# Attention by summation by parts: products replaced by differences of values, the last value added on the way out of PSUM

## The chip, the core and the metric

The program runs on one core of one Trainium2 chip. The metric is device time of one execution in microseconds; the kernel before takes 2888.41 us (median of three runs, 2887.97 to 2892.59). The core has five engines that work at once: PE (TensorE, matrix products, with its weight loads PEld), DVE (VectorE), ACT (ScalarE), POOL (GpSimd) and SP, which here only issues transfers. Each takes its own instructions in order and waits on semaphores for the others.

## What is computed

A decoder trunk of two layers over 1040 positions (16 learned ones and 1024 given) of width 1024: a Mamba-2 mixer with a conv FFN, and then a layer of stick-breaking attention with a conv FFN. The change is in the attention alone, 16 heads of 64 columns. Cut to what matters:

```
logits   = q k^T / 8                                  # for s < t only
log_keep = log_sigmoid(-logits)                       # 0 where s >= t
later    = reversed exclusive cumulative sum of log_keep over s
w        = exp(log_sigmoid(logits) + later)           # 0 where s >= t
out      = w v
```

So the weight of position s is b(s) times the product of all k(s') with s' > s, where b = sigmoid(logit) and k = sigmoid(-logit) = 1 - b, and k is 1 where s >= t. With P(s), the product of k from s to the end, the weight is b(s) P(s+1). As b = 1 - k, it is also P(s+1) - P(s).

## The kernel before

The attention works on 8 pairs of heads. The 1040 positions are cut into 9 chunks of 116 (the last has 112), and these into 3 tiles of three chunks (348, 348 and 344 positions). For each pair there are 18 steps: chunk i of queries against key tile jj, from the chunk's own tile down to tile 0. A step (`weigh`) has these pieces, with the names that rows of the profile show:

- PE: four matmuls `lg` (two heads, queries and keys in two parts each) into a PSUM tile of two banks, which there is once (twice for the last nine steps of the last pair).
- ACT: two sigmoids out of `lg`, with the query's factor as scale (`rt[2]` and `rt[1]`): k into `kp` and b into `bt` (L1398).
- POOL: sets the column behind the last of `kp` to 1 (L1393); where the tile is the chunk's own, it puts 1 into `kp` and 0 into `bt` at s >= t (L1403).
- DVE: two scans that run backward over `kp` and leave the products in it (L1407, one a head, starting from the product that the step before ended with), and then the product `bt` times `kp` shifted by one column (L1408).

Three steps later `turn` transposes the weights on PE (`wT`, L1421, into a ring of three PSUM banks) and ACT copies them out (`wt`, L1425). For every second chunk `values` then multiplies them with the values (`po`, L1436), ACT copies the result out (`o`, L1443) and sends it to memory for the layer behind.

The values get there so: a projection `pj` (L164 to L166) gives a tile of them with channels on partitions, ACT copies it out (`v`, L1324), and two steps later `place` turns it on PE (`pv`, into the same ring of three banks) and DVE multiplies it with the token's norm factor `rt[0]` on the way out (L1365). Keys (L1322) are multiplied by that factor `r` straight out of PSUM instead.

The projections of the next pair (queries, keys, values, 24 matmuls per kind and tile, in halves of 12) are put between the steps by hand: `halves` says which half stands at which step, and the last pair has such work only up to its step 7. In the attention the order of PE, DVE, ACT and POOL is that in which the program is written. Outside of it a scheduler sets the order. Behind the attention follows the output projection (`acc`), and then the second FFN.

Of the kernel before, what the change touches and what calls it, by code (L numbers as in the profile page):

```python
# [68 lines left out]
class Trunk:  # L69
# [1199 lines left out]
    def heads(self, u, p, pool):  # L1269
# [4 lines left out]
        class Pair:  # L1274
# [4 lines left out]
            def load(me, kind):  # L1279

                src, gain = {"k": (a["w_kv"][p], "kv_norm"), "q": (a["w_q"][p], "sb_norm"), "v": (a["w_kv"][PAIRS + p], "kv_norm")}[kind]
                w32 = self.wp.tile([P, 1024], F32, tag="w32", name=self.nm("w32"))
                nc.sync.dma_start(w32, src)
                if kind == "k":
                    me.ks = [self.Q("k", F32R), self.Q("k", F32R)]
                elif kind == "v":
                    me.v = pool.tile([P, 9, P], F32, tag="v", name=self.nm("v"), bufs=2)

                def scale_halves():
                    for x in range(2):  # L1290
                        v = w32[:, D // 2 * x : D // 2 * (x + 1)].rearrange("p (k c) -> p k c", c=P)
                        g = self.par(gain, KD // 2 * x, KD // 2).unsqueeze(2).to_broadcast([P, KD // 2, P])
                        nc.vector.tensor_tensor(v, v, g, op=ALU.mult)

                def part_halves():
                    me.w[kind] = [self.wp.tile([P, 1024], F32R, tag=t, name=self.nm(t)) for t in ("wh", "wl")]
                    halves = [[t[:, D // 2 * x : D // 2 * (x + 1)] for t in (w32, *me.w[kind])] for x in range(2)]
                    for w, wh, _ in halves:
                        nc.scalar.activation(wh, w, AF.Copy)
                    for w, wh, wl in halves:  # L1300
                        nc.vector.tensor_tensor(wl, w, wh.bitcast(F32), op=ALU.subtract)

                return [scale_halves, part_halves]

            def half(me, kind, j, h):
# [18 lines left out]
                nc.scalar.activation(t[:, :n], ps[:, :n], AF.Copy)  # L1324
                me.late.append((j, t))
# [29 lines left out]
            def place(me):  # L1355

                todo, me.old, me.late = me.old, me.late, []
                for j, t in todo:
# [5 lines left out]
                    for x, y, m in ((0, 3, CB),) if j < 2 else ((0, 2, CB), (2, 3, CH[8][1])):  # L1364
                        nc.vector.tensor_tensor(v[:m, 3 * j + x : 3 * j + y], pv[:m, x * P : y * P].rearrange("p (c d) -> p c d", d=P),  # L1365
                                                self.rt[0][:m, 3 * j + x : 3 * j + y].unsqueeze(2).to_broadcast([m, y - x, P]), op=ALU.mult)
# [3 lines left out]
    def token_factors(self, r, pool):  # L1370

        nc = self.nc
        self.rt = [pool.tile([P, 9], F32, tag=f"rt{x}", name=self.nm("rt"), bufs=1) for x in range(3)]
        for j, (s0, _) in enumerate(TT):
# [4 lines left out]
            for x, y, m in ((0, 3, CB),) if j < 2 else ((0, 2, CB), (2, 3, CH[8][1])):  # L1379
                src = ps[:m, : 3 * P].rearrange("p (c d) -> p c d", d=P)[:, x:y, 0]  # L1380
                for t, scale in zip(self.rt, (1.0, SCALE, -SCALE)):
                    nc.vector.tensor_scalar(t[:m, 3 * j + x : 3 * j + y], src, scale, None, op0=ALU.mult)

    def weigh(self, i, jj, qd, ks, prev, pool, ps):
# [6 lines left out]
        kp = pool.tile([P, 2, TW], F32, tag="kp", name=self.nm("kp"), bufs=3)  # L1391
        bt = pool.tile([P, 2, TW], F32, tag="bt", name=self.nm("bt"), bufs=4)
        nc.gpsimd.memset(kp[:nt, :, m : m + 1], 1.0)  # L1393
# [3 lines left out]
        for t, r in ((kp, self.rt[2]), (bt, self.rt[1])):  # L1397
            nc.scalar.activation(t[:nt, :, :m], ps[:nt, :, :m], AF.Sigmoid, scale=r[:nt, i : i + 1])  # L1398
        if jj == j:

            for t, fill in ((kp, 1.0), (bt, 0.0)):
                own = t[:nt, :, c0 : c0 + nt]
                nc.gpsimd.affine_select(out=own, in_=own, compare_op=ALU.is_gt, fill=fill, base=0, pattern=[[0, 2], [-1, nt]], channel_multiplier=1)  # L1403
        for a in range(2):
            rev = kp[:nt, a, : m + 1][:, ::-1]
            init = 1.0 if jj == j else prev[0][:nt, a, 0:1]
            nc.vector.tensor_tensor_scan(rev, rev, self.one[:nt].to_broadcast([nt, m + 1]), init, ALU.mult, ALU.mult)  # L1407
        nc.vector.tensor_tensor(bt[:nt, :, :m], bt[:nt, :, :m], kp[:nt, :, 1 : m + 1], op=ALU.mult)  # L1408
        prev[0] = kp
        return [bt[:, a] for a in range(2)]  # L1410

    def turn(self, i, jj, bt, wt):
# [4 lines left out]
        for a in range(2):  # L1417
            pt = self.sm("wT")
            for x, c in enumerate(blocks):
                ns = CH[c][1]  # L1420
                nc.tensor.transpose(pt[:ns, x * CB : x * CB + nt], bt[a][:nt, x * CB : x * CB + ns], self.ident[:nt, :nt])  # L1421
# [5 lines left out]
    def values(self, p, chunks, v, os, od):  # L1427
# [10 lines left out]
        for b, (i, _) in enumerate(chunks):  # L1438
# [4 lines left out]
            nc.scalar.activation(os[p][:, c0 : c0 + nt], po[:, b * CB : b * CB + nt], AF.Copy)  # L1443
# [3 lines left out]
    def attention(self, u, pool):  # L1447
# [15 lines left out]
        def flush(n):  # L1463
            if ready and (ready[-1][1] % 2 or ready[-1][1] == 8):
                p = ready[0][0]
                self.values(p, [(i, wts.pop((p, i))) for _, i in ready], pairs[p].v, os, od)
                ready.clear()
            if len(turns) > n:
                p, i, jj, bt = turns.pop(0)
                if jj == i // 3:  # L1470
                    wts[p, i] = [self.Q("wt")[:, : 9 * CB].rearrange("p (c t) -> p c t", t=CB) for _ in range(2)]
                self.turn(i, jj, bt, wts[p, i])
# [14 lines left out]
        for p in range(PAIRS):  # L1487
            prev = None
            for n, (i, jj) in enumerate(steps):
# [7 lines left out]
                bt = self.weigh(i, jj, now[0].qd[i // 3], now[0].ks, prev, pool, ps)  # L1497
# [14 lines left out]
                turns.append((p, i, jj, bt))  # L1512
# [182 lines left out]
```

## Time and profile before

| | us |
|---|---|
| median of the runs | 2888.41 |
| the profiled execution | 2887.39 |
| its span | 2885.7 |
| attention's first step (first `lg`) | at 1562 |
| last step's `po` begins | at 2079 |
| PE busy over the span | 2825.6 (98%) |
| DVE busy over the span | 2108.5 (73%) |
| ACT busy over the span | 1638.6 (57%) |
| POOL busy over the span | 664.1 (23%) |

Times in rows are microseconds from the start of the span. A row of a group names the line, the engine, the operation, output and inputs by the program's names, the count, and then the busy time, the mean of one in ns, and the idle time before it with what ended it. Matmuls are pipelined, so that PE's busy time holds some waiting, and short pieces of PE work look longer than the room they take. A row of a window gives its two ends, its length, for each engine the busy time with the count of instructions, and then PE's granted clock as a share of full speed, the share of the DMA engines and GB/s. A pair takes 65.6 us between the pairs in the middle.

### The profile page before, as it was taken

Reading aid. Unit: us, or ns where it says so; the run is one execution under the profiler, and the core shown is the slowest. Engines: PE = TensorE matmul, PEld = TensorE weight load, DVE = VectorE, ACT = ScalarE, POOL = GpSimd, SP = SyncE. Lnnn points to the kernel's source line nnn. Section 1 sums busy time; section 2 is a strip of 40 time slices with the busy share of each in tenths; the row PEclk is TensorE's granted clock in tenths of the full one; section 3 lists DMA queues with packets and bytes.
Section 4 is the critical chain, followed back from the end, with each engine's and each line's share of the span. In section 5 each row is a group of like instructions: output and inputs, shape, how many; then the busy total and the mean of one; then the engine's idle time right before and its main releaser. Section 6 shows DMA issues by size and latency. Waiting matters only on the chain.

```text
span 2885.7 us, 55788 instructions
## 1 busy us (share of the span) xinstructions
PE 2825.6 (98%) x21808; PEld 2706.5 (94%) x21808; DVE 2108.5 (73%) x3872; ACT 1638.6 (57%) x3203; POOL 664.1 (23%) x662
## 2 busy tenths in 40 slices
PE   8999999999999999999999999999999999999998
PEld 5989898989999999999999999999898999999888
DVE  5685868776587656568987888888769565657895
ACT  5576767773255555555435776777736555555442
POOL 0000000000005666650000111221101766662000
PEclk9999999999999999999999999999999999999999
DMA  6233333314221222226142222222341222225331
GB/s 169 79 111 87 117 94 110 106 57 157 86 95 67 80 76 81 76 97 212 53 136 79 64 62 67 67 62 57 132 152 52 88 75 80 78 78 190 110 110 59
DMA packets 134135, 274.76 MB, mean 95 GB/s; under 512 B 16464, under 2 KB 68304, under 8 KB 133872
## 3 DMA queue, kind: packets, MB, share of 16 engines
q1 hardware_dynamic: 128560, 260.26, 28.4%
q10 hardware_dynamic: 4048, 6.36, 0.6%
q0 software_dynamic: 1264, 4.57, 0.4%
q8 instruction: 172, 2.82, 0.4%
q14 instruction: 91, 0.75, 0.1%
HBM read 203.02 MB, written 53.21 MB: 89 GB/s over the span
## 4 chain that ended last, share of the span: by engine, by line
PE 73%; DVE 8%; issue 5%; ACT 5%; POOL 1%; DMA 0%; DVEq 0%; POOLq 0%; ACTq 0%; SPq 0%
PE p L166 10%; PE p L164 10%; PE p L165 10%; PE acc L166 8%; PE acc L165 8%; PE acc L164 8%; PE pj L164 4%; PE pj L165 4%; PE pj L166 4%; PE po L1436 2%; PE lg L1396 2%; PE wT L1421 2%; DVE kp L1407 1%; ACT D L614 1%; DVE bl L917 1%
## 5 line engine op out<-in xcount | busy, mean ns | idle before, releaser
L164 PE MATMUL pj<-uh,wh 128*128 128x348 f32 (+2 forms) x1536 | 502.8, 328 | 7.3 <-DVE xbc L292 6.1
L165 PE MATMUL pj<-ul,wh 128*128 128x348 f32 (+2 forms) x1536 | 495.5, 323 | 0.0
L166 PE MATMUL pj<-uh,wl 128*128 128x348 f32 (+2 forms) x1536 | 492.6, 321 | 0.0
L164 PE MATMUL p<-bh,fh 128*128 128x262 f32 (+1 forms) x1408 | 400.1, 285 | 8.5 <-DVE p L1041 4.7
L165 PE MATMUL p<-bl,fh 128*128 128x262 f32 (+1 forms) x1408 | 401.3, 285 | 0.4
L166 PE MATMUL p<-bh,fl 128*128 128x262 f32 (+1 forms) x1408 | 399.8, 285 | 0.3 <-DVE fl L972 0.3
L165 PE MATMUL p<-bl,wh 128*128 128x262 f32 (+1 forms) x1056 | 301.4, 285 | 1.5 <-DVE bl L917 1.5
L164 PE MATMUL p<-bh,wh 128*128 128x262 f32 (+1 forms) x1056 | 301.7, 286 | 1.0 <-ACT bh L916 1.0
L166 PE MATMUL p<-bh,wl 128*128 128x262 f32 (+1 forms) x1056 | 302.1, 286 | 0.0
L164 PEld LDWEIGHTS pj<-uh,wh 128*128 128x128 f32 x1536 | 289.2, 188 | 12.6 <-issue 7.8
L165 PEld LDWEIGHTS pj<-ul,wh 128*128 128x128 f32 x1536 | 289.6, 189 | 1.8 <-issue 0.6
L166 PEld LDWEIGHTS pj<-uh,wl 128*128 128x128 f32 x1536 | 289.0, 188 | 0.5
L164 PEld LDWEIGHTS p<-bh,fh 128*128 128x128 f32 x1408 | 268.1, 191 | 9.8 <-DVE p L1041 5.1
L292 DVE SCALAR_TENSOR_TENSOR c<-p,params,c 128x260 f32<-128x260 f32 (+1 forms) x440 | 208.2, 482 | 92.1 <-ACT c L288 90.2
L165 PEld LDWEIGHTS p<-bl,fh 128*128 128x128 f32 x1408 | 267.4, 190 | 1.6 <-DVE bl L917 1.4
L166 PEld LDWEIGHTS p<-bh,fl 128*128 128x128 f32 x1408 | 267.4, 190 | 0.7 <-DVE fl L972 0.5
L972 POOL TENSOR_TENSOR fl<-x,fh 128x1024 fp32r<-128x1024 f32 x80 | 192.5, 2406 | 253.3 <-ACT fh L971 253.3
L1041 DVE TENSOR_TENSOR p<-p,ft 128x262 f32<-128x262 f32 (+1 forms) x176 | 76.5, 436 | 215.3 <-ACT ft L1038 124.2
L165 PE MATMUL acc<-gl,wh 128*128 128x260 f32 (+1 forms) x672 | 211.1, 319 | 0.0
L166 PE MATMUL acc<-gh,wl 128*128 128x260 f32 (+1 forms) x672 | 208.3, 319 | 0.0
L165 PEld LDWEIGHTS p<-bl,wh 128*128 128x128 f32 x1056 | 202.2, 191 | 2.1 <-DVE bl L917 2.1
L164 PE MATMUL acc<-gh,wh 128*128 128x260 f32 (+1 forms) x672 | 204.0, 319 | 0.0
(313 smaller groups left out, 7507.0 us busy)
## 6 DMA issues: line engine op xcount, KB each, us to landing
w<-in_w_up SPq DMA_DIRECT2D x92, 512.0 KB
w<-in_w_down SPq DMA_DIRECT2D x44, 512.0 KB
w<-in_w_in SPq DMA_DIRECT2D x40, 512.0 KB
E<-ea_d SPq DMA_DIRECT2D x32, 464.0 KB
D<-acs_d SPq DMA_DIRECT2D x32, 420.5 KB
g<-c SPq DMA_DIRECT2D x88, 130.0 KB
g<-c SPq DMA_DIRECT2D x88, 128.0 KB
b<-g SPq DMA_DIRECT2D x16, 520.0 KB
```

Of the source, the lines that this page charges most:

```text
L164: mm(out, wh, uh, start=first, stop=False, skip_group_check=joins)
L165: mm(out, wh, ul, start=False, stop=False, skip_group_check=joins)
L166: mm(out, wl, uh, start=False, stop=last, skip_group_check=joins)
L292: nc.vector.scalar_tensor_tensor(to, ps[:, o + i : o + i + n], wcol(i), out, op0=ALU.mult, op1=ALU.add)
L614: nc.scalar.activation(dk[:, i], dk[:, i], AF.Relu, scale=-1.0, bias=self.cols[:n, 1, cc, h0 + i : h0 + i + 1])
L917: tt(hl[1], x, hl[0].bitcast(F32), op=ALU.subtract)
L972: (self.nc.vector if b < 2 else self.nc.gpsimd).tensor_tensor(lo[:, :n], t, hi[:, :n].bitcast(F32), op=ALU.subtract)
L1041: add = lambda o, x, y: tt(o[:, :N], x[:, :N], y[:, :N], op=ALU.add)
L1396: nc.tensor.matmul(ps[:nt, a, :m], part[:, c0 : c0 + nt], ks[a][:, s0 : s0 + m], start=x == 0, stop=x == 1)
L1407: nc.vector.tensor_tensor_scan(rev, rev, self.one[:nt].to_broadcast([nt, m + 1]), init, ALU.mult, ALU.mult)
L1421: nc.tensor.transpose(pt[:ns, x * CB : x * CB + nt], bt[a][:nt, x * CB : x * CB + ns], self.ident[:nt, :nt])
L1436: nc.tensor.matmul(po[64 * a : 64 * a + 64, w], v[: CH[c][1], c, 64 * a : 64 * a + 64], wt[a][: CH[c][1], c, :nt], start=x == 0, stop=x == ...
```

## The change

The sum of (P(s+1) - P(s)) v(s) over s is summed by parts: it is v at the last position minus the sum of P(s) (v(s) - v(s-1)), with v(-1) = 0. Since a row's P is 1 from s = t on, the last position of the query's own chunk serves as the last for its whole chunk. So the products P themselves, as the scan leaves them, are transposed and multiplied with v(s-1) - v(s), and v of the chunk's last position, which is a column of 128 channels, is added as the bias of ACT's copy out of PSUM.

In `weigh` this leaves out `bt`: its sigmoid, its POOL select, and the DVE product; the column of ones and its memset go too. `kp` has 6 buffers in place of 3 (and of 4 for `bt`). For the values, DVE multiplies the projection by `r` out of PSUM, where ACT copied before, POOL puts the last value of the tile ahead into column 0, DVE subtracts neighbours into another tile (`dv`), and POOL copies three columns (`ends`) aside for the bias. Those differences are turned on PE as the values were, and ACT copies them out where DVE multiplied by `rt[0]`. One table of token factors is left of three.

```
                 elif kind == "v":
                     me.v = pool.tile([P, 9, P], F32, tag="v", name=self.nm("v"), bufs=2)
+                    me.ends = pool.tile([P, 9], F32, tag="ends", name=self.nm("ends"), bufs=2)
...
-                nc.scalar.activation(t[:, :n], ps[:, :n], AF.Copy)
-                me.late.append((j, t))
+                front = me.ends[:, 3 * j - 1 : 3 * j] if j else self.zero[:, :1]
+                nc.gpsimd.tensor_copy(t[:, :1], front)
+                nc.vector.tensor_tensor(t[:, 1 : n + 1], ps[:, :n], u[KD][:, o:e], op=ALU.mult)
+                d = self.tmp("dv")
+                nc.vector.tensor_tensor(d[:, :n], t[:, :n], t[:, 1 : n + 1], op=ALU.subtract)
+                for i in range(3):
+                    last = CB * i + CH[3 * j + i][1]
+                    nc.gpsimd.tensor_copy(me.ends[:, 3 * j + i : 3 * j + i + 1], t[:, last : last + 1])
+                me.late.append((j, d))
...
-                        nc.vector.tensor_tensor(v[:m, 3 * j + x : 3 * j + y], pv[:m, x * P : y * P].rearrange("p (c d) -> p c d", d=P),
-                                                self.rt[0][:m, 3 * j + x : 3 * j + y].unsqueeze(2).to_broadcast([m, y - x, P]), op=ALU.mult)
+                        nc.scalar.activation(v[:m, 3 * j + x : 3 * j + y], pv[:m, x * P : y * P].rearrange("p (c d) -> p c d", d=P), AF.Copy)
...
-        kp = pool.tile([P, 2, TW], F32, tag="kp", name=self.nm("kp"), bufs=3)
-        bt = pool.tile([P, 2, TW], F32, tag="bt", name=self.nm("bt"), bufs=4)
-        nc.gpsimd.memset(kp[:nt, :, m : m + 1], 1.0)
+        kp = pool.tile([P, 2, TW], F32, tag="kp", name=self.nm("kp"), bufs=6)
...
-        for t, r in ((kp, self.rt[2]), (bt, self.rt[1])):
-            nc.scalar.activation(t[:nt, :, :m], ps[:nt, :, :m], AF.Sigmoid, scale=r[:nt, i : i + 1])
+        nc.scalar.activation(kp[:nt, :, :m], ps[:nt, :, :m], AF.Sigmoid, scale=self.rt[:nt, i : i + 1])
...
-            nc.vector.tensor_tensor_scan(rev, rev, self.one[:nt].to_broadcast([nt, m + 1]), init, ALU.mult, ALU.mult)
-        nc.vector.tensor_tensor(bt[:nt, :, :m], bt[:nt, :, :m], kp[:nt, :, 1 : m + 1], op=ALU.mult)
+            nc.vector.tensor_tensor_scan(rev, rev, self.one[:nt].to_broadcast([nt, m]), init, ALU.mult, ALU.mult)
         prev[0] = kp
-        return [bt[:, a] for a in range(2)]
+        return [kp[:, a] for a in range(2)]
...
-            nc.scalar.activation(os[p][:, c0 : c0 + nt], po[:, b * CB : b * CB + nt], AF.Copy)
+            nc.scalar.activation(os[p][:, c0 : c0 + nt], po[:, b * CB : b * CB + nt], AF.Identity, bias=ends[:, i : i + 1])
```

PE's instructions in the attention stand in the same order as before, with other inputs, and so do SP's transfers. Behind the attention the scheduler exchanges two matmuls of the output projection and some rows of the second FFN's first rounds. Two engines change at places that the prediction speaks of.

On DVE, the last pair's steps 9 to 12 before (a scan is printed as SCALAR_TENSOR_TENSOR, x2 for the two heads):

```order
L1407 SCALAR_TENSOR_TENSOR kp_24274<-kp_24274,one 116x117 x2
L1408 TENSOR_TENSOR bt_24275<-bt_24275,kp_24274 116x2x116
L1365 TENSOR_TENSOR v_23453<-pv_24290,rt_17627 116x256
L1365 TENSOR_TENSOR v_23453<-pv_24290,rt_17627 112x128
L1407 SCALAR_TENSOR_TENSOR kp_24307<-kp_24307,kp_24274,one 116x349 x2
L1408 TENSOR_TENSOR bt_24308<-bt_24308,kp_24307 116x2x348
L1407 SCALAR_TENSOR_TENSOR kp_24332<-kp_24332,kp_24307,one 116x349 x2
L1408 TENSOR_TENSOR bt_24333<-bt_24333,kp_24332 116x2x348
L1407 SCALAR_TENSOR_TENSOR kp_24355<-kp_24355,one 116x233 x2
L1408 TENSOR_TENSOR bt_24356<-bt_24356,kp_24355 116x2x232
```

The same pair's steps 7 to 12 now, with the last value tile's two instructions in step 7 (`wl` of L158 is a split of an output weight that the scheduler put there before too):

```order
L1409 SCALAR_TENSOR_TENSOR kp_23723<-kp_23723,one 116x348 x2
L1327 TENSOR_TENSOR v_23746<-pj_23695,r_16957 128x344
L158 TENSOR_TENSOR wl_24322<-w_3443_24319,wh_24321 128x768
L1329 TENSOR_TENSOR dv_23749<-v_23746 128x344
L1409 SCALAR_TENSOR_TENSOR kp_23765<-kp_23765,kp_23723,one 116x348 x2
L1409 SCALAR_TENSOR_TENSOR kp_23807<-kp_23807,one 116x116 x2
L1409 SCALAR_TENSOR_TENSOR kp_23835<-kp_23835,kp_23807,one 116x348 x2
L1409 SCALAR_TENSOR_TENSOR kp_23856<-kp_23856,kp_23835,one 116x348 x2
L1409 SCALAR_TENSOR_TENSOR kp_23875<-kp_23875,one 116x232 x2
```

From step 8 on nothing but scans is left on DVE until the attention's end: the products and the two multiplications of L1365 are gone from between them.

On POOL, steps of a middle pair around a value tile, now (before, two selects and a memset stood at such a step, and nothing for the values):

```order
L1405 AFFINE_SELECT kp_18491<-kp_18491 116x2x116
L1326 COPY v_18519<-ends_18076 128x1
L1332 COPY ends_18076<-v_18519 128x1 x3
L1405 AFFINE_SELECT kp_18538<-kp_18538 116x2x116
L1405 AFFINE_SELECT kp_18573<-kp_18573 116x2x116
```

The three copies into `ends` wait for DVE's multiplication of L1327, and the next step's select stands behind them.

More of the change, by code (lines that the diff above doesn't have):

```diff
@@ L1372, in token_factors @@
         nc = self.nc
-        self.rt = [pool.tile([P, 9], F32, tag=f"rt{x}", name=self.nm("rt"), bufs=1) for x in range(3)]
+        self.rt = pool.tile([P, 9], F32, tag="rt", name=self.nm("rt"), bufs=1)
         for j, (s0, _) in enumerate(TT):
@@ L1380, in token_factors @@
                 src = ps[:m, : 3 * P].rearrange("p (c d) -> p c d", d=P)[:, x:y, 0]
-                for t, scale in zip(self.rt, (1.0, SCALE, -SCALE)):
-                    nc.vector.tensor_scalar(t[:m, 3 * j + x : 3 * j + y], src, scale, None, op0=ALU.mult)
+                nc.vector.tensor_scalar(self.rt[:m, 3 * j + x : 3 * j + y], src, -SCALE, None, op0=ALU.mult)
     def weigh(self, i, jj, qd, ks, prev, pool, ps):
@@ L1420, in turn @@
                 ns = CH[c][1]
-                nc.tensor.transpose(pt[:ns, x * CB : x * CB + nt], bt[a][:nt, x * CB : x * CB + ns], self.ident[:nt, :nt])
+                nc.tensor.transpose(pt[:ns, x * CB : x * CB + nt], kp[a][:nt, x * CB : x * CB + ns], self.ident[:nt, :nt])
             spans = [(0, len(blocks), CB)] if CH[blocks[-1]][1] == CB else [(0, 2, CB), (2, 3, CH[8][1])]
@@ L1425, in turn, with values @@
                 nc.scalar.activation(wt[a][:ns, 3 * jj + x : 3 * jj + y, :nt], src, AF.Copy)
-    def values(self, p, chunks, v, os, od):
+    def values(self, p, chunks, v, ends, os, od):
         nc = self.nc
@@ L1465, in flush @@
                 p = ready[0][0]
-                self.values(p, [(i, wts.pop((p, i))) for _, i in ready], pairs[p].v, os, od)
+                self.values(p, [(i, wts.pop((p, i))) for _, i in ready], pairs[p].v, pairs[p].ends, os, od)
                 ready.clear()
             if len(turns) > n:
-                p, i, jj, bt = turns.pop(0)
+                p, i, jj, kp = turns.pop(0)
                 if jj == i // 3:
                     wts[p, i] = [self.Q("wt")[:, : 9 * CB].rearrange("p (c t) -> p c t", t=CB) for _ in range(2)]
-                self.turn(i, jj, bt, wts[p, i])
+                self.turn(i, jj, kp, wts[p, i])
                 if jj == 0:
@@ L1496, in attention @@
                 ps = both(more if p + 1 == PAIRS and n > 8 and n % 2 else self.lp)
-                bt = self.weigh(i, jj, now[0].qd[i // 3], now[0].ks, prev, pool, ps)
+                kp = self.weigh(i, jj, now[0].qd[i // 3], now[0].ks, prev, pool, ps)
                 todo, late = late, []
@@ L1511, in attention @@
                 flush(LAG)
-                turns.append((p, i, jj, bt))
+                turns.append((p, i, jj, kp))
         while turns or ready:
```

9 lines of the change are left out of this document (4 added, 5 removed).

## The prediction

> **What bounds the kernel now.** I began with the page, for the engines, and went from there to the windows of the attention, since the change touches nothing else. A window's row gives the two ends, the length, the busy times of PE, PEld, DVE, ACT and POOL, and the granted clock.
>
> ```profile
> span 2885.7 us, 55788 instructions
> PE 2825.6 (98%) x21808; PEld 2706.5 (94%) x21808; DVE 2108.5 (73%) x3872; ACT 1638.6 (57%) x3203; POOL 664.1 (23%) x662
> ```
> ```profile
> 1560.00:1625.00 65.00, 63.87 (x490) 61.41 (x489) 53.81 (x92) 44.30 (x91) 11.50 (x36) 1.00 0.25 66
> 1690.00:1755.00 65.00, 64.85 (x565) 61.76 (x564) 54.80 (x83) 45.24 (x101) 12.95 (x36) 1.00 0.23 62
> 2015.00:2080.00 65.00, 58.56 (x570) 53.16 (x570) 53.59 (x76) 48.77 (x112) 14.33 (x36) 0.99 0.35 112
> 2053.00:2084.00 31.00, 24.54 (x250) 20.67 (x249) 25.43 (x36) 23.98 (x57) 6.10 (x14) 0.94 0.48 169
> 2068.00:2073.00 5.00, 3.41 (x40) 2.73 (x41) 4.76 (x7) 4.32 (x10) 1.49 (x4) 1.00 0.49 176
> ```
>
> For a middle pair (second row) PE is busy 64.85 of 65 us; DVE has 10 us and ACT 20 us to spare. What the change takes from DVE and ACT there is hidden under PE already. The last pair is another matter (third and fourth rows): its projections end at step 7, and from 2053 on PE is busy 24.54 of 31 us. In that tail it is DVE that has no room, 4.76 of 5 us in the fifth row. So the question is what stands on DVE in the tail, and what PE waits for in the rest. The waits of the attention, all of PE's and, for the middle pairs from 1690 to 2000, those of its weight loads:
>
> ```profile
> PE wT L1421 <- DVE bt L1408: 2.8, 3, 1.9
> PE wT L1421 <- ACT wt L1425: 2.5, 5, 0.8
> PE wT L1421 <- DVE v L1365: 2.1, 2, 1.1
> ...
> PEld po L1436 <- issue: 5.2, 24, 0.2
> PEld wT L1421 <- issue: 2.9, 19, 0.2
> PEld wT L1421 <- DVE v L1365: 1.7, 5, 0.4
> PEld lg L1396 <- ACT bt L1398: 1.5, 8, 0.2
> ```
>
> Each names something that the change removes or takes from DVE (`bt` twice, `v` of L1365 twice), but all are small: the whole change has some ten microseconds to win, whatever it saves on the engines.
>
> **The change part by part.** What goes and what comes, from the groups of the attention:
>
> ```profile
> L1408 DVE TENSOR_TENSOR bt<-bt,kp 116x232 f32<-116x232 f32 (+3 forms) x144 | 109.9, 763 | 17.1
> L1398 ACT ACTIVATE bt<-lg,rt 116x232 f32<-116x232 f32 (+3 forms) x144 | 108.2, 752 | 0.0
> L1403 POOL TENSOR_SCALAR_AFFINE_SELECT bt<-bt 116x232 f32<-116x232 f32 (+1 forms) x72 | 49.4, 686 | 6.5 <-ACT bt L1398 4.5
> L1393 POOL MEMSET kp<- 116x2 f32 (+1 forms) x143 | 11.1, 98 | 113.7 <-DVE kp L1407 111.8 <-DVE bt L1408 1.8
> L1365 DVE TENSOR_TENSOR v<-pv,rt 116x384 f32<-116x384 f32 (+2 forms) x32 | 13.7, 450 | 0.0
> L1324 ACT ACTIVATE v<-pj 128x348 f32<-128x348 f32 (+1 forms) x24 | 11.3, 473 | 8.5 <-PE pj L166 8.5
> L1322 DVE TENSOR_TENSOR k<-pj,r 128x348 f32<-128x348 f32 (+1 forms) x22 | 11.3, 516 | 0.5
> L1334 DVE TENSOR_TENSOR klo<-k,k 128x348 fp32r<-128x348 f32 (+1 forms) x22 | 12.8, 581 | 0.0
> L1425 ACT ACTIVATE wt<-wT 116x348 f32<-116x348 f32 (+5 forms) x304 | 103.8, 402 | 22.2 <-PE wT L1421 18.5 <-ACT o L1443 3.2
> L388 POOL COPY h<-zero 128x2 f32<-128x2 f32 x8 | 2.5, 359 | 22.4 <-PE pj L166 22.4
> L822 POOL COPY r<-zero 128x2 f32<-128x2 f32 x1 | 3.0, 2966 | 145.6 <-ACT yh L174 145.6
> ```
>
> DVE loses 109.9 + 13.7 us and gets, per value tile (24 of them), a multiplication out of PSUM like L1322 and a subtraction like L1334: 24 x (0.516 + 0.581) = 26 us. ACT loses 108.2 + 11.3 and gets 32 copies of the kind of L1425, 32 x 0.40 = 13 us. POOL loses 60.5 and gets 96 copies of one column, for which L388 is the nearest row: 96 x 0.36 = 34 us. PE's and SP's lists stay. A scan over one column less is worth nothing that a row shows, and the copy with a bias in place of a plain one lies on ACT, which waits for `po` there anyway.
>
> None of those savings counts where PE is full. Three places are left.
>
> *A. The tail of the last pair.* Its rows (first three: groups of 2053 to 2084; then rows of the timeline with start and length, the two of `po` being 36 equal matmuls, and between them a window of the half clock):
>
> ```profile
> L1408 DVE TENSOR_TENSOR bt<-bt,kp 116x696 f32<-116x696 f32 (+4 forms) x10 | 8.1, 811 | 1.2
> L1365 DVE TENSOR_TENSOR v<-pv,rt 116x256 f32<-116x256 f32 (+1 forms) x2 | 0.6, 350 | 0.0
> L1407 DVE TENSOR_TENSOR_SCAN kp<-kp,kp,one 116x349 f32<-116x349 f32 (+1 forms) x14 | 12.6, 940 | 0.0
> ...
> 2077.25 0.88 DVE L1408 TENSOR_TENSOR bt<-bt,kp 112x696 f32<-112x696 f32 x1
> 2078.28 0.76 PE L1421 MATMUL wT<-ident,bt 112*116 112x112 f32 x6 [1.85 <-DVE bt L1408]
> 2078.97 3.60 PE L1436 MATMUL po<-wt,v 116*64 116x112 f32 x36
> ...
> 2079.00:2082.00 3.00, 3.00 (x33) 3.00 (x34) 1.38 (x3) 1.72 (x5) 0.00 (x0) 0.50 0.00 0
> ...
> 1706.57 1.95 PE L1436 MATMUL po<-wt,v 116*64 116x112 f32 x36
> ```
>
> DVE's chain there loses ten products and the two multiplications between them, 8.1 + 0.6 = 8.7 us; the last of the products is itself what PE waits for at the end. PE's side bounds it: it idles 31.00 - 24.54 = 6.5 us, and the last 36 matmuls ran at a granted clock of 0.50 and took 3.60 in place of 1.95, which is 1.65 more. Both together, 8.1 us, is what PE can gain without its short pieces lying closer. The lower of the two sides is 8.1; I take 0.3 off for the scans (two of 0.94 a step) and PE's ring of three banks, which now end close to each other: **7.8 us**. Bounds: half of the idle time and no clock, 3.2; all of DVE's 8.7 and the clock, 10.3.
>
> On the clock: the trace shows it halved right behind an idle time of 1.85 us. The Trainium skill (TensorE: Matmul & The Clock Gate, "Part 1: The HAM clock gate") has it fall after an idle window of about 3.4 us, and by that this gap alone would not do it; a shorter gap would then promise nothing, and the term would be 6.2 without the 1.65.
>
> *B. The middle.* Twice a pair the loads of `lg` wait about 0.2 us for the second sigmoid, since one PSUM tile holds `lg`, and once the transposes wait 0.35 us for DVE's multiplication of `v` to free a bank of the ring:
>
> ```profile
> 1731.88 1.11 PE L1421 MATMUL wT<-ident,bt 116*116 116x116 f32 x6
> 1735.36 0.76 PE L1421 MATMUL wT<-ident,bt 116*116 116x116 f32 x6
> 1728.33 0.88 DVE L1408 TENSOR_TENSOR bt<-bt,kp 116x696 f32<-116x696 f32 x1
> ```
>
> The first row is the one behind a value tile, 1.11 - 0.76 = 0.35 us longer than the next. DVE came to L1365 only after the step's scans and product; ACT will come to its copy right behind the step's one sigmoid. The loads' rows, (1.7 + 1.5) us over 310 us, make 0.68 per pair of 65.6 us, or 4.8 for seven pairs. PE itself shows no idle time there, so that part of it is hidden: between 0 and 4.8 I take **3.0 us**, nearer the upper end since the 0.35 is seen in PE's own row.
>
> *C. The start.* PE's waits from 1562 to 1625 are one:
>
> ```profile
> PE wT L1421 <- DVE v L1365: 1.0, 1, 1.0
> ```
>
> PE's window from 1560 to 1625 has 65.00 - 63.87 = 1.1 us of idle time, nearly all of it this wait for the first value tiles' multiplication (the other 1.1 of the 2.1 above is in the tail). **1.0 us**, between 0 and 1.1.
>
> Sum: 7.8 + 3.0 + 1.0 = 11.8 us, bounds 3.2 and 16.2. The profiled execution took 2887.39 (its span and 1.7 around it), so it would come to 2875.6; the median of the runs lies 1.0 above that execution, and so the forecast is **2876.6 us**, 0.4% faster. What comes behind passes the gain on: PE is busy there as soon as the output projection begins, and its loads are issued as buffers come free, not at fixed times. The exchanged rows in the second FFN I put at nothing; this is the cheapest error to make here, a microsecond either way.
>
> **New waits.** DVE's subtraction waits for POOL's copy into column 0, which stands ahead of the projection's end and so is done. POOL's three copies wait for DVE's multiplication, and the next step's select is behind them. That delays a scan at most by 0.52 + 3 x 0.36 = 1.6 us. In the middle there is time for it: the product of 1728.33 ended at 1729.21 and was transposed at 1735.36, 6.1 us later. `dv` has two steps until it is turned.
>
> **The rivals.** (1) *The tail gives little:* PE's transposes, ACT's copies and the ring of three banks take turns, and PE's 2.5 us of waits for `wt` grow as DVE's shrink. For it speaks ACT, 4.32 of 5 us in the tail; against it, that ACT loses a sigmoid of 0.75 a step there. Then A is 3.2, B and C 1.0 together: 2888.4 - 4.2 = 2884.2, no change that can be told.
>
> (2) *More of the middle:* the "issue" waits ahead of `po` and `wT`, (5.2 + 2.9) us in 310, or 1.7 a pair, are late semaphores of ACT and DVE and go as well: 12 us more, 2864.6. Against it: each is the same 0.2 us, wherever it stands, which looks like a cost of changing from one kind of matmul to another.
>
> (3) *Slower, by POOL:* the copies of one column take far longer than 0.36 us beside DVE's work; the selects spread from 0.39 to 1.06 us (least, median and most in ns), and the one copy of L822 shows 2.97.
>
> ```profile
> L1403 POOL TENSOR_SCALAR_AFFINE_SELECT kp<-kp x72: 386/548/1061, 1565.6 to 2067.4; 116x232 f32<-116x232 f32 x64, 112x224 f32<-112x224 f32 x8
> ```
>
> Up to (6.1 - 0.5) / 4 = 1.4 us a copy the slack takes it. At the middle between the rows, 1.7 us, a tile is 0.5 + 4 x 1.7 - 6.1 = 1.2 us late, 29 us for 24 tiles, and less 8.8 for A and C the time is 2908.6. The Trainium skill (Advanced Engine Details and Errata, "VectorE Performance Modes") speaks for it: GpSimd shares VectorE's second port into SBUF, and each blocks the other. The selects' spread agrees with that; but the products, which read two tensors, are what goes.
>
> (4) The remaining case is a loss behind the attention, by the exchanged rows or loads that come late: some 3 to 8 us that eat most of the gain, 2881 to 2888.
>
> **How the numbers follow.** The forecast has 0.68, rival 1 0.13, rival 2 0.07, rival 3 0.05, the rest 0.07. About 0.2%, or 5.8 us, is what a measurement tells from no change, so "faster" is below 2882.6: forecast and rival 2, and a little of the rest, 0.76. "Same" is rival 1 and most of the rest, 0.18; "slower" 0.06. The range must leave out no more than 0.2: from 2870 (the bounds' sum, 16.2, gives 2872.2, and some of rival 2) to 2887 (rival 1, and most of the rest).
>
> **What would show it.** In the profile after: in the tail from the end of the projections PE idle by less than 2 us, DVE's row with scans alone, and the 36 `po` of the end at 1.95 us (A); no wait of `wT` for `v` and none of `lg` for a second sigmoid, with pairs of 65.2 us in place of 65.6 (B); the first window without its 1.0 us (C). DVE's busy time falls to about 2011 us, ACT's to 1532, POOL's to 638. It would be wrong if the tail shows PE waiting for `wt` as long as it waited for `bt`, if selects stand behind `ends` with scans waiting for them on the path, or if a pair of the middle is longer than 65.6 us.

## The result, and the profile after

The changed kernel takes 2872.56 us (median; 2871.28 to 2874.41), the kernel before 2888.19 in the runs beside it: a ratio of 0.9944, with a 95% interval from 0.9932 to 0.9955. The forecast was 2876.6. The gain is 15.6 us, where 11.8 was expected; the profiled execution (2871.28 us) is the one whose trace is read here.

The head of the page, after:

```profile
span 2869.6 us, 54962 instructions
PE 2815.9 (98%) x21808; PEld 2705.5 (94%) x21808; DVE 2003.3 (70%) x3736; ACT 1559.2 (54%) x3067; POOL 619.1 (22%) x542
```

Three windows show where the time went: up to the attention's first `lg`, from there to the first matmul of the output projection (`acc`), and the rest. First before, then after (columns as in the prediction: ends, length, busy time of PE, PEld, DVE, ACT and POOL, granted clock, DMA share, GB/s):

```profile
0.00:1562.05 1562.05, 1527.66 (x11538) 1470.20 (x11539) 1107.56 (x2126) 879.26 (x1662) 287.83 (x211) 0.99 0.32 102
1562.05:2082.50 520.45, 512.03 (x4444) 485.53 (x4441) 437.75 (x656) 365.85 (x803) 103.50 (x287) 1.00 0.24 67
2082.50:2885.70 803.20, 785.93 (x5832) 750.74 (x5830) 563.20 (x1090) 393.51 (x739) 272.73 (x164) 0.99 0.29 99
```
```profile
0.00:1562.70 1562.70, 1528.17 (x11538) 1470.59 (x11539) 1107.31 (x2126) 879.12 (x1662) 287.71 (x210) 0.99 0.32 102
1562.70:2065.82 503.12, 502.55 (x4443) 484.37 (x4441) 329.57 (x520) 286.65 (x667) 58.53 (x168) 1.00 0.24 70
2065.82:2869.60 803.78, 785.23 (x5832) 750.58 (x5830) 566.41 (x1092) 393.41 (x739) 272.90 (x164) 0.99 0.29 99
```

The attention is 17.33 us shorter; the stretches around it are 0.65 and 0.58 longer. The second columns hold the lesson of this case. PE does the same matmuls in both, yet its *busy* time in the attention falls by 9.48 us, more than its idle time, which falls from 8.42 to 0.57. Of the 9.48, 1.65 is the half clock of the last `po` (3.60 us in place of 1.95); the rest, some 7.8 us, were waits that the profile counted as busy time of PE.

The same windows as in the prediction, after; the last one is the tail, whose end has moved from 2082.5 to 2065.8 (2053 before corresponds to about 2045 now):

```profile
1560.00:1625.00 65.00, 65.00 (x507) 63.60 (x506) 43.96 (x74) 35.62 (x77) 7.57 (x24) 1.00 0.26 69
1690.00:1755.00 65.00, 65.00 (x572) 62.86 (x572) 41.98 (x66) 36.09 (x84) 7.62 (x24) 1.00 0.23 62
2044.00:2066.00 22.00, 21.43 (x249) 18.98 (x247) 16.27 (x23) 17.80 (x49) 2.63 (x4) 1.00 0.65 234
```

PE idles nowhere in the first two, and 0.57 us in the 22 of the tail. Its last pieces there, from the timeline (start and length):

```profile
2061.57 2.44 PE L1422 MATMUL wT<-ident,kp 112*116 112x112 f32 x18
2063.94 1.95 PE L1437 MATMUL po<-wt,v 116*64 116x112 f32 x36
```

The last 18 transposes run without a break, and the last 36 `po` take 1.95 us: full clock. The waits of PE and its loads from 1690 to 2000 (PE itself has none any more):

```profile
PEld po L1437 <- issue: 5.4, 25, 0.2
PEld wT L1422 <- issue: 2.6, 17, 0.2
PEld wT L1422 <- DVE kp L1409: 0.3, 2, 0.2
```

The waits for `v`, for the second sigmoid and for the product are gone. The "issue" waits stand as they stood. Two groups of the attention that are new:

```profile
L1444 ACT ACTIVATE o<-po,ends 128x116 f32<-128x116 f32 (+1 forms) x72 | 23.1, 354 | 95.1 <-PE po L1437 91.4 <-ACT o L1444 3.2
L1332 POOL COPY ends<-v 128x1 f32<-128x1 f32 x72 | 22.0, 348 | 83.4 <-DVE v L1327 83.4
```

POOL's copies of one column into `ends` take 0.348 us, as the nearest row had promised; the 24 into column 0 take 0.18.

For the experiments one measure is finer than the run time: the attention's length in the profile, from the first `lg` of a pair to the first of the next, and in the last pair to the first `acc`. Between kernels that differ only elsewhere it repeats to 0.02 us or so, while the time up to the attention varies by up to 5.6 us between profiled executions. All lengths, less those of the changed kernel (448.54 us for pairs 1 to 7, 54.58 for the last):

| kernel | pairs 1 to 7 | last pair | time, us (median) |
|---|---|---|---|
| changed | 0 | 0 | 2872.56 |
| before | +8.87 | +8.46 | 2888.19 |
| `e1_product` | +6.84 | +8.92 | 2888.42 |
| `e2_sigmoid` | 0.00 | +4.06 | 2875.41 |
| `e3_v_dve` | 0.00 | -0.04 | 2873.64 |
| `e4_fill` (the kernel before) | +8.78 | +6.22 | 2885.42 |
| `e5_tail` | 0.00 | +7.64 | 2880.33 |
| `e12_tail_product` | 0.00 | +6.98 | 2879.81 |
| `e6_middle` | +10.04 | 0.00 | 2882.42 |
| `e11_scale_early` | +8.61 | +7.04 | 2888.30 |
| `e10_scale_pool` | +31.55 | +6.68 | 2912.39 |
| `e9_kp4` | 0.00 | 0.00 | 2872.18 |
| `e7_pool10` | +2.22 | +0.06 | 2877.63 |
| `e8_pool30` | +161.14 | +24.66 | 3057.99 |

The 8.87 of pairs 1 to 7 divide into 1.25 for step 3 of the first pair (steps are counted from 0), the one with the wait for `v` (C), and 7.6 for the rest, about 1.1 a pair (B). The last pair is A.

### The profile page after: what moved, and what is told of

Its sections match the earlier page's. It is cut to its first block, busy times and chain, and to the rows that moved or that the text cites. A ratio compares the mean times of both kernels' runs of the same rounds, so it can differ in the third digit from the quotient of the medians.

```text
span 2869.6 us, 54962 instructions
## 1 busy us (share of the span) xinstructions
PE 2815.9 (98%) x21808; PEld 2705.5 (94%) x21808; DVE 2003.3 (70%) x3736; ACT 1559.2 (54%) x3067; POOL 619.1 (22%) x542
## 4 chain that ended last, share of the span: by engine, by line
PE 81%; DVE 6%; ACT 4%; issue 1%; DMA 0%; ACTq 0%; DVEq 0%; SPq 0%
PE p L166 10%; PE p L165 10%; PE p L164 10%; PE acc L166 8%; PE acc L165 8%; PE acc L164 8%; PE pj L164 5%; PE pj L165 5%; PE pj L166 5%; PE lg L1400 3%; PE po L1437 3%; PE wT L1422 3%; ACT D L614 1%; DVE xbc L292 1%; DVE bl L917 1%
## 5 line engine op out<-in xcount | busy, mean ns | idle before, releaser
L164 PEld LDWEIGHTS p<-bh,wh 128*128 128x128 f32 x1056 | 202.1, 191 | 2.1 <-ACT bh L916 1.2
```

Of the source, the lines that this page charges most:

```text
L164: mm(out, wh, uh, start=first, stop=False, skip_group_check=joins)
```

## The experiments

Where a sigmoid, a product or another instruction is put back, its result is either a copy by ones or read by nobody, so that the numbers computed stay the same and only the engine's time is spent.

### Which engine's relief counts

**The product alone.** In every step DVE multiplies the scans' result by ones into another tile, which is what PE turns; the second sigmoid stays out.

```
-        kp = pool.tile(..., bufs=6)
+        kp = pool.tile(..., bufs=4)
...
-        return [kp[:, a] for a in range(2)]
+        bt = pool.tile([P, 2, TW], F32, tag="bt", name=self.nm("bt"), bufs=4)
+        nc.vector.tensor_tensor(bt[:nt, :, :m], kp[:nt, :, :m], self.one[:nt].unsqueeze(2).to_broadcast([nt, 2, m]), op=ALU.mult)
+        return [bt[:, a] for a in range(2)]
```

> The changed kernel with a DVE product put back behind the scans: the products are multiplied by ones into a second tile, and PE transposes that one, as it did before (kp has 4 buffers, the second tile 4). The second sigmoid stays out. Theory 'DVE on the path': in the tail DVE again has 8.1 us of products between the scans and PE waits for most of it, and in the middle the query splits (qs) come late again, 0.28 us a pair: 5 to 9 us slower than the changed kernel, 2878 to 2882. Rival 'the second sigmoid was it' (ACT's time in the tail, and the PSUM tile of lg that it kept): 0 to 2 us slower, up to 2875.

Measured: 2888.42 us, a ratio of 0.9999 [0.9989, 1.0008]. All of the gain in time is gone, through DVE's product alone (in the attention 15.76 of the 17.33 us), about twice the theory's 5 to 9. The query splits hardly come late again, which the theory had at 0.28 us a pair: from 1690 to 2000 the loads wait for them once, 0.2 us. In the middle nearly all of the loss, 0.9 us a pair, falls in one step, step 9. Its waits between 1690 and 2000, and then what ACT and PE do there (timeline; in brackets the idle time before and what ended it):

```profile
PEld wT L1424 <- ACT wt L1428: 4.7, 5, 1.0
PE wT L1424 <- ACT wt L1428: 3.3, 5, 0.7
```
```profile
1726.01 1.24 ACT L1300 ACTIVATE wh<-w 128x512 fp32r<-128x512 f32 x2 [3.77 <-DVE w L1294]
1728.56 0.81 PE L1424 MATMUL wT<-ident,bt 116*116 116x116 f32 x6 [0.68 <-ACT wt L1428]
```

ACT stands idle for 3.77 us at `wh`, a split of the next pair's weights, which waits for DVE's scaling of them (L1294). Behind it in ACT's order stand the copies `wt` that free the ring for PE. With the product away the same row of the changed kernel waits less, and PE not at all:

```profile
1721.46 1.23 ACT L1300 ACTIVATE wh<-w 128x512 fp32r<-128x512 f32 x2 [1.16 <-DVE w L1294]
```

**The second sigmoid alone**, unread, in every step:

```
+        b2 = pool.tile([P, 2, TW], F32, tag="b2", name=self.nm("b2"), bufs=2)
+        nc.scalar.activation(b2[:nt, :, :m], ps[:nt, :, :m], AF.Sigmoid, scale=self.rt[:nt, i : i + 1])
```

> The changed kernel with a second sigmoid out of lg put back on ACT in each step, into a tile that nobody reads. Theory 'DVE on the path, and the sigmoid only where it keeps lg': lg waits 0.2 us twice a pair again, 2.7 us for seven pairs, and the tail loses 1 to 3 us since ACT is full there: 3 to 6 us slower than the changed kernel, 2875.5 to 2878.5. Rival 'the second sigmoid was it': 8 us or more slower, 2880 and up. If it costs nothing, the waits of lg for the second sigmoid were no loss.

Measured: 2875.41 us, 0.9949 [0.9932, 0.9966]. In pairs 1 to 7 it costs 0.00, where the theory had 2.7: the waits of `lg` "for the second sigmoid" were not the sigmoid's doing as long as DVE is in time. In the tail it costs 4.06 us, more than the theory's 1 to 3 and all of it from step 10 on, so that the theory's total was nearly met by luck. Most of it falls in the last four steps at some 0.73 each, about the length of a sigmoid (0.75 in the mean): there ACT sets the pace, busy 13.35 us of 15 (PE 12.21):

```profile
2053.00:2068.00 15.00, 12.21 (x141) 10.53 (x138) 10.63 (x13) 13.35 (x30) 0.77 (x2) 1.00 0.55 187
```

**The values' copy out of PSUM on DVE**, as before, with ones as the factor:

```
-                        nc.scalar.activation(v[:m, ...], pv[:m, ...], AF.Copy)
+                        nc.vector.tensor_tensor(v[:m, ...], pv[:m, ...], self.one[:m]...to_broadcast([m, y - x, P]), op=ALU.mult)
```

> The changed kernel with the turned value differences copied out of PSUM by DVE, multiplied by one in the shape of the old multiplication, in place of ACT's copy. Theory 'DVE came late to it because the product stood ahead': with the product gone DVE is in time, 0 to 1 us slower than the changed kernel, 2872.5 to 2873.5, and no wait of the transposes for it. Rival 'DVE is the wrong engine for it at any load': the 0.38 us a pair and the 1.25 us of the first pair come back, 3.9 us slower, 2876.5.

Measured: 2873.64 us, 0.9946 [0.9931, 0.9961]; no pair differs by more than 0.04 us. So, without the product ahead of it, DVE makes that copy in time, and the wait of `wT` for `v` (B and C in the prediction) stays away. The first experiment shows the other half: there the product is back and ACT makes the copy, and step 3 of the first pair and step 10 of pairs 2 to 7 lose 0.00 and 0.03 us (the kernel before: 1.26 and 0.38). Each of the two changes takes the wait away by itself, at least in the first pair, where step 3 comes ahead of every other loss.

### The tail

**Sigmoid and product back in the last pair's steps 8 to 17 only** (steps counted from 0, in `weigh` under `old = p == 7 and n >= 8`), and then **the product alone** in the same place (the same without the sigmoid's line):

```
+        if old:
+            bt = pool.tile([P, 2, TW], F32, tag="bt", name=self.nm("bt"), bufs=4)
+            nc.scalar.activation(bt[:nt, :, :m], ps[:nt, :, :m], AF.Sigmoid, scale=self.rt[:nt, i : i + 1])
...
+        nc.vector.tensor_tensor(bt[:nt, :, :m], kp[:nt, :, :m], self.one...to_broadcast([nt, 2, m]), op=ALU.mult)
+        return [bt[:, a] for a in range(2)]
```

> The changed kernel, with the second sigmoid and the product (by ones, into the tile that PE transposes) put back in steps 8 to 17 of the last pair alone; kp has 4 buffers. The product alone, in all steps, cost 15.9 us (2888.4 in place of 2872.6), 8.9 of it in the last pair's rows, and the second sigmoid alone 4.1 there. Theory 'two engines, each of them enough to fill the tail': together they cost no more than the worse of them, 8 to 9 us, 2881, and the middle's pairs stay at 64.5 us. Rival 'their times add': 13 us, 2885.5.

> The changed kernel with the product alone put back in steps 8 to 17 of the last pair (kp with 4 buffers); it completes the four cases of the tail: neither, the sigmoid alone (4.1 us longer, in a run that had it in all steps), both (7.6). Theory 'each of the two engines fills the tail by itself, and what is over goes into the last step': 5 to 8 us longer, 2878 to 2880.5, mostly in the last two steps, with the half clock behind PE's wait. Rival 'DVE alone would keep up, only both together are late': under 3 us, below 2875.5.

Measured: both 2880.33 us (0.9971 [0.9960, 0.9982]), the product alone 2879.81 (0.9969 [0.9958, 0.9980]). With the second sigmoid alone, above, that makes a square for the last pair: neither 0, sigmoid 4.06, product 6.98, both 7.64 us. They don't add: each engine alone fills the tail, and by these runs taking away one of the two would have brought 0.7 us (the product stays) or 3.6 (the sigmoid stays). The product alone, last steps:

```profile
2066.96 1.77 DVE L1412 TENSOR_TENSOR_SCAN kp<-kp,kp,one 112x348 f32<-112x348 f32 x2
2068.83 0.88 DVE L1416 TENSOR_TENSOR bt<-kp,one 112x696 f32<-112x696 f32 x1
...
2069.86 0.76 PE L1428 MATMUL wT<-ident,bt 112*116 112x112 f32 x6 [1.91 <-DVE bt L1416]
2070.55 3.42 PE L1443 MATMUL po<-wt,v 116*64 116x112 f32 x36
```

Two scans and a product are 2.65 us a step, and PE waits 1.91 for the last and then pays the lower clock again, 3.42 for 1.95.

**The clock.** The kernel before, with 18 transposes of the identity, read by nobody, in PE's last gap:

```
+            if len(turns) == 1:
+                fill = both(self.lp)
+                for x in range(18):
+                    nc = self.nc
+                    nc.tensor.transpose(fill[:, x % 2, :P], self.ident, self.ident)
```

> The kernel before, with 18 transposes of the identity into a PSUM tile that nobody reads, put on PE ahead of the last step's transposes, where PE idled 1.85 us. Theory 'the idle time halved the clock': the last 36 po matmuls take 1.95 us in place of 3.60 at a granted clock of 1.00, and the kernel is 1.3 to 1.7 us faster than before, 2886.6. Rival 'a gap as short as this does not halve it; it is something else ahead of it': they stay at about 3.6 us and the time stays, 2888.2 or a little more.

Measured: 2885.42 us, 0.9989 [0.9979, 0.9998].

```profile
2077.32 2.13 PE L1518 MATMUL lg<-ident 128*128 128x128 f32 x18
2079.34 0.76 PE L1421 MATMUL wT<-ident,bt 112*116 112x112 f32 x6
2080.03 1.38 PE L1436 MATMUL po<-wt,v 116*64 116x112 f32 x24
...
2082.23 0.80 PE L1436 MATMUL po<-wt,v 116*64 116x112 f32 x12
```
```profile
2079.00:2082.00 3.00, 3.00 (x40) 2.62 (x38) 2.43 (x7) 2.08 (x6) 0.00 (x0) 1.00 0.00 0
```

The clock stays at 1.00 where it was 0.50. The last step, from its `lg` to the end of `po`, (2069.74 to 2083.03) takes 13.3 us, and 0.9 of that (2081.33 to 2082.23) is output projection, which got in between; less that it is 12.4, against 13.9 before (2068.68 to 2082.57). So the half clock came from the gap and costs 1.5 us, where the prediction had 1.65. The run as a whole gained more than that: its median is 3.5 us below the kernel before beside it (2888.91), and in the profiles the stretch from the first `lg` to the end is 3.15 us shorter. What brought the rest, behind the attention, was not traced. The Trainium skill (TensorE: Matmul & The Clock Gate, "Part 1: The HAM clock gate") has the clock fall after an idle window of about 3.4 us; here 1.85 us of idle time with short pieces of work ahead of it did it, and the measurement decides. A gap alone is not the whole rule, though: in the run with the product alone a gap of 1.81 us (before 2059.31) left the 60 `po` behind it at full clock (3.20 us). The first two rows below are of the kernel before, the others of the product alone in the tail:

```profile
2075.58:2078.99 3.41, 1.56 (x15) 1.13 (x14) 2.42 (x3) 1.57 (x7) 0.00 (x0) 1.00 0.00 0
2078.99:2082.40 3.41, 3.41 (x37) 3.26 (x36) 1.38 (x3) 1.73 (x5) 0.00 (x0) 0.50 0.00 0
...
2057.16:2060.57 3.41, 1.60 (x13) 1.19 (x11) 2.96 (x4) 2.36 (x6) 0.46 (x1) 1.00 0.88 310
...
2067.40:2070.81 3.41, 1.50 (x18) 1.16 (x18) 2.21 (x3) 1.23 (x4) 0.00 (x0) 1.00 0.00 0
2070.81:2074.22 3.41, 3.41 (x37) 3.13 (x34) 1.38 (x3) 1.67 (x6) 0.00 (x0) 0.50 0.02 5
```

In both kernels the half clock fills a stretch of 3.41 us, and in the 3.41 us ahead of it PE is busy for 1.56 or 1.50 us, less than half. The third row holds the gap of 1.81 (its ends are counted back from 2070.81 in steps of 3.41); it has 1.60 us busy, hardly more, and full clock behind it. Whether the busy share of such stretches decides, and where the limit lies, no run here tries.

### The middle

**Sigmoid and product back in all pairs but the last** (`old = p < 7` in the edit above):

> The same two put back in all steps of the pairs before the last, and not in the last one. Theory 'the middle's gain is DVE's alone, since a second sigmoid alone cost the middle nothing': pairs of 65.4 to 65.7 us as with the product alone, 0.9 to 1.1 longer than the changed kernel's, 6.5 to 8.5 us in all, 2880. Rival 'the second sigmoid's hold on lg comes on top once DVE is late': 1.3 us a pair and more, 2882 and up.

Measured: 2882.42 us, 0.9979 [0.9969, 0.9988]; the seven pairs lose 1.32 to 1.67 us each, 10.04 in all, nearly all of it in step 9. It is the rival that came true.

```profile
PE wT L1429 <- ACT wt L1433: 3.3, 5, 0.7
PEld lg L1400 <- ACT bt L1405: 2.0, 6, 0.4
```

The wait of the first experiment is there again, 0.7 us, and the wait of `lg` for the second sigmoid comes on top. The sigmoid that costs nothing alone costs 0.46 a pair in the mean once the product makes DVE late.

**Is it the scaling of the weights?** If the loss of 0.9 us goes from DVE's L1294 through ACT's `wh` and `wt` to PE, it must change when that scaling moves. Two kernels, both the first experiment plus: the scaling on POOL; the query's weights scaled one step earlier on DVE.

```
-                        nc.vector.tensor_tensor(v, v, g, op=ALU.mult)
+                        nc.gpsimd.tensor_tensor(v, v, g, op=ALU.mult)
```
```
-        loads = {(-1, 4): "k", (-1, 6): "q", (-1, 9): "v"}
+        loads = {(-1, 4): "k", (-1, 5): "q", (-1, 9): "v"}
...
-                for f in todo + chores[:1]:
+                now_many = {6: 2, 7: 0}.get(n, 1)
+                for f in todo + chores[:now_many]:
```

> The changed kernel with the product put back in all steps (as in the first of these runs), and the scaling of the next pair's weights by their gains, which ACT's split of them waits for, moved from DVE to POOL. Theory 'DVE's lateness reaches PE through ACT, which waits in order for the scaled weights while the copies of the transposes stand behind': the 0.95 us a pair that the product cost in step 9 goes, pairs of 64.6 us or less than 0.3 above, and the tail keeps its 8.9 us: 2881.5. Rival 'PE waits for the product itself': pairs of 65.5 us still, 2888.4. Further, POOL's scaling could be late itself: then step 9 is longer by another wait, named so.

> The changed kernel with the product put back in all steps, as in the first run, and the next pair's query weights loaded and scaled one step earlier: DVE's scaling in step 6 in place of step 7, ACT's split of them in step 8 as before. DVE has as much to do as in the first run. Theory 'DVE's lateness reaches PE through ACT, which waits in order for the scaled weights': the 0.95 us of step 9 goes, pairs of 64.5 to 64.8 us, the tail keeps its 8.9 us: 2881 to 2883. Rival 'PE waits for the product, or DVE's load as such': pairs of 65.5 us as in the first run, 2888.4.

Measured: on POOL 2912.39 us (1.0088 [1.0071, 1.0105]), earlier 2888.30 (1.0002 [0.9993, 1.0012]). Neither brought the 0.9 back: for the second it is the rival that came true, for the first the case named last. On POOL one multiplication takes 1.33 us (0.68 on DVE) and is itself what is late; the path is the same, only longer:

```profile
ACT wh L1300 <- POOL w L1294: 25.7, 8, 5.4
PE wT L1424 <- ACT wt L1428: 13.4, 4, 3.4
```

With the scaling earlier, that path is closed and the loss isn't: PE's wait for `wt` is gone from the waits of 1690 to 2000, and another stands in its place, in the same step, somewhat longer.

```profile
PE pv L1371 <- DVE dv L1329: 5.1, 5, 1.1
```

So the theory that one wait is the cause fell. As the first experiment's trace shows it, DVE is late as a whole around that step (two scans of 348 columns, product, `v`, `dv`, the weights' scaling, with no gap between them), and it seems that whichever of its results is wanted first makes PE wait.

None of these runs is the kernel before again. That one lost 0.15 us in step 9, and 0.38, 0.27 and 0.22 in steps 10, 16 and 17 (means of pairs 2 to 7); with the product back, alone or with the sigmoid, step 9 loses 0.91 or 1.35, and steps 10, 16 and 17 lose 0.03 or less. The changed kernel's DVE also has `v` and `dv` ahead of step 9, 1.0 us that the kernel before did not have there. So what is shown is that the changed kernel's DVE has no room for the product. That the product stood behind each of the four waits of the kernel before is read from its rows; the run for it, the kernel before with its product left out, was not made.

### POOL's slack, and a control

**Ten and thirty memsets on POOL** behind each value tile's copies (the edit with ten):

```
+                slow = pool.tile([P, TW], F32, tag="slow", name=self.nm("slow"), bufs=1)
+                for _ in range(10):
+                    nc.gpsimd.memset(slow, 0.0)
```

> The changed kernel with ten memsets of 128x352 on POOL behind the three copies into ends of each value tile; by the memset of 128x128 (0.23 us) and that of 128x4 (0.10 us) of the kernel before they take 4.7 us together. Theory 'POOL has slack: a select may be late by the time to the next step that needs one and some 6 us more': 0 to 1 us, 2872.6 to 2873.6. Rival 'the select behind the copies is close to the path' (the prediction's slower case): from 1.4 us a copy on, that is 4 x 1.4 = 5.6 us a tile, it would begin to show; 4.7 + 0.7 stays just below, and a loss above 5 us would say that it is closer.

> The same with thirty memsets, 14 us a value tile. Theory 'slack of a step (3 to 5 us) and 6 us more': the scan of the next own tile comes 3 to 5 us late at two of three value tiles, 16 tiles, 50 to 80 us in all: 2922 to 2952. If it is under 2880, the slack is far larger than the prediction worked out.

Measured: 2877.63 us (0.9961 [0.9949, 0.9972]) and 3057.99 (1.0588 [1.0567, 1.0609]). A run of ten memsets stands 4.44 us in POOL's row, one of thirty 13.44. With ten the expected 0 to 1 us was missed, 5.1 in the median and 2.28 in the attention. Pairs 2 to 7 lose nothing, though scans wait more for selects (108.6 us in all, 76.6 in the changed kernel). The first pair loses 2.22 us; its first two value tiles come 1.6 us apart, and the memsets of one hold up POOL's copy into column 0 for the next, for which DVE waits 3.74:

```profile
1580.43 0.52 DVE L1329 TENSOR_TENSOR dv<-v 128x348 f32<-128x348 f32 x1 [3.74 <-POOL v L1326]
```

In the profiled execution the rest of the time is the varying stretch ahead of the attention (first `lg` at 1567.44, 4.7 us later) and 1.4 us behind it. With thirty, scans wait for selects behind the memsets, and PE for what comes of them (1690 to 2000):

```profile
DVE kp L1412 <- POOL kp L1408: 130.4, 22, 13.9
PE pv L1374 <- DVE dv L1329: 15.7, 3, 5.2
```

The size was missed by far: 185 us over the changed kernel, or 7.7 a tile. POOL's work at a tile is then 0.52 + 4 x 0.35 + 13.44 = 15.4 us, so that the slack, in the sense of rival 3, comes to 15.4 - 7.7 = 7.7 us, where the prediction read 6.1 from one tile. With ten memsets, 6.4 us, it covers them, as measured from the second pair on. These are two points; they bound the slack and don't prove the mechanism tile by tile.

**Control.** The changed kernel with the buffers of `kp` at 4, since the runs above have 4 where the change has 6:

> The changed kernel with 4 buffers for kp in place of 6 and nothing else, as a control for the runs that put the product back with 4. Theory 'the buffers are no part of the gain': 0 to 0.5 us, 2872.6, each pair as long as the changed kernel's. Rival 'the longer ring frees ACT's sigmoids': a tile is then freed by the transposes one step before it is written again, and the tail loses 2 us or more.

Measured: 2872.18 us, 0.9943 [0.9929, 0.9958], no pair different. The buffers play no part.

## Why the prediction was right, and where it was off

**A, the tail: 7.8 expected, 8.46 measured.** The two parts were right: idle time of 6.46 us fell to 0.57, and the clock gave 1.5 of its 1.65. Some 1.1 us (8.46 - 5.89 - 1.5) were waits that counted as busy, so that the 0.3 taken off for scans and ring was not needed. The reason was half right. The prediction named DVE as the engine without room; the square shows ACT in the same place, at 4.06 us by itself. Had the change taken only DVE's product out of the tail, it would have won 3.6 us there, and rival 1, with 3.2, would have come true in that part.

**B, the middle: 3.0 expected, 7.6 measured, above its upper bound of 4.8.** This is the term that was mis-sized. That the loads' waits were the place to look is right. A middle pair gained 0.16 in step 9, 0.38 in step 10, 0.28 in step 16 and 0.22 in step 17, 1.04 in all, and in each of the four a load waits about as long in the kernel before:

```profile
1729.23 0.60 PEld L1396 LDWEIGHTS lg<-k,qs 128*116 128x116 f32 x4 [0.16 <-ACT bt L1398]
1732.48 0.29 PEld L1421 LDWEIGHTS wT<-ident,bt 116*116 116x116 f32 x3 [0.36 <-DVE v L1365]
...
1750.99 0.19 PEld L164 LDWEIGHTS pj<-uh,wh 128*128 128x128 f32 x1 [0.32 <-DVE qs L1350]
1756.89 0.48 PEld L1396 LDWEIGHTS lg<-k,qs 128*116 128x116 f32 x4 [0.21 <-ACT bt L1398]
```

Two errors made the term small. First, "PE itself shows no idle time there, so that part of it is hidden": it was not. These waits of the loads were paid in full; PE's busy time, with its modelled ends, covers them. Second, a row of the same view (1690 to 2000) was left out, the wait in step 16:

```profile
PEld pj L164 <- DVE qs L1350: 1.2, 4, 0.3
```

With the 1.7 and 1.5 that the prediction used it makes 4.4 us in 310, 0.93 a pair, 6.5 for seven pairs: near the 7.6, with no discount. The row of `lg` was also put down to the second sigmoid alone. In the kernel before ACT waits for DVE's `k`, and the sigmoids behind it come late; PE then starts `lg` 0.75 us after `wT` in place of 0.53:

```profile
1754.18 0.49 ACT L1333 ACTIVATE k<-k 128x348 fp32r<-128x348 f32 x1 [1.45 <-DVE k L1322]
...
1755.98 0.86 ACT L1398 ACTIVATE bt<-lg,rt 112x696 f32<-112x696 f32 x1
```
```profile
1753.01 0.76 PE L1421 MATMUL wT<-ident,bt 116*116 116x116 f32 x6
1753.54 0.87 PE L1396 MATMUL lg<-k,qs 128*112 128x348 f32 x4
...
1756.14 0.76 PE L1421 MATMUL wT<-ident,bt 116*116 116x116 f32 x6
1756.89 0.62 PE L1396 MATMUL lg<-k,qs 128*116 128x116 f32 x4
```

The runs agree that it takes both: `lg` waits neither with the sigmoid alone nor with the product alone, and with both it waits 2.0 us.

**C, the start: 1.0 expected, 1.25 measured**; the loads' wait there is 1.3. The wait went, and for the reason given, ACT's copy, as the first experiment shows; by the third the product's end alone would have done it too.

**New waits: none, as expected.** The columns' copies take 0.348 us (0.36 assumed), and the slack held.

**The rivals.** Rival 1 (the tail gives little) and rival 3 (POOL) did not come true, for the reasons above. Rival 2's "issue" waits stayed, 8.0 us from 1690 to 2000 against 8.1, so that they look like no late semaphores of the engines that were relieved. What rival 2 guessed was right in one respect, that the middle had more to give, but it came from other rows. Behind the attention 0.58 us were lost, within the microsecond allowed.

**Busy times.** DVE came to 2003 us (2011 expected), POOL to 619 (638; its selects became shorter too, see below), ACT to 1559 (1532). ACT's 27 us have two sources. The copy with a bias takes 0.354 us where the plain one took 0.264 (the row below, of before), 7 us in all; the prediction put it at nothing. For the path that looks right, since ACT waits 91.4 us for `po` there, but no run has that copy alone. The rest is overlap: rows of one engine that stand close overlap, so that savings added up from groups are larger than what the busy time loses. By groups ACT lost 108.2 + 11.3 - 12.6 (`v` out of `pv`) - 6.9 = 100 us, and its busy time in the attention fell by 365.85 - 286.65 = 79 us. The Trainium skill (ScalarE: Activation LUTs, "What ACT_TABLE_LOAD costs") has both, about 93 ns for an operand of one value a partition and 93 ns of overlap; the trace agrees with the first, 0.090 us.

```profile
L1443 ACT ACTIVATE o<-po 128x116 f32<-128x116 f32 (+1 forms) x71 | 16.2, 264 | 66.1 <-PE po L1436 62.8 <-ACT o L1443 3.3
```

The change left PE busy 65.00 of 65 us in a middle pair, and none of the runs here is faster than it beyond their spread. Whether PE has anything left to win there is open: its loads still show 8.0 us of "issue" waits in 310.

## What to carry to other kernels

A matmul engine shown as busy for the whole of a window may still be waiting: add up the waits of its weight loads, all rows that name an engine, and count them in full, as came out here (the "issue" rows stayed). Where two engines both fill a stretch without slack, relieving one alone brings less (here 0.7 or 3.6 of 7.64 us), so measure each alone and both before crediting one. And a wait named after one engine (a copy, a sigmoid) may be the lateness of another that came through an in-order queue: putting the suspected work back by itself tells them apart, as far as the kernel around it is still the same.

## What was unexpected of the hardware

- The time up to the attention, with the same instructions, differed by up to 5.6 us between profiled executions (first `lg` at 1562.05 to 1567.66 us), while pairs inside the attention repeated to about 0.02 us.
- PE's clock was halved for 3.41 us behind a gap of 1.85 us (before) and of 1.91 (the product alone in the tail), not behind one of 1.81, and filling the gap with transposes that nobody reads kept it.
- POOL's selects on `kp` became faster, 0.673 us before and 0.468 after, with 0.637 where only DVE's product was put back (0.469 with the 4 buffers alone). So DVE's product lengthens POOL's selects. It is not all that does: with the second sigmoid alone put back they take 0.387, and DVE's work is the same; what stands beside a select was not sorted out. The changed kernel's group, and that of the first experiment:

```profile
L1405 POOL TENSOR_SCALAR_AFFINE_SELECT kp<-kp 116x232 f32<-116x232 f32 (+1 forms) x72 | 33.7, 468 | 620.9 <-ACT kp L1401 349.0 <-DMA qs<-qs 271.9
```
```profile
L1405 POOL TENSOR_SCALAR_AFFINE_SELECT kp<-kp 116x232 f32<-116x232 f32 (+1 forms) x72 | 45.9, 637 | 573.5 <-ACT kp L1401 301.5 <-DMA qs<-qs 271.9
```
